# Hybrid decoder trunk on one core: down stages in whole products, the norm's end in two parts, squares on ScalarE, and the first two weight slots side by side

## The chip, the cores and the metric

The kernel runs on one core of a Trainium2 chip. The metric is device time in microseconds of one execution; the median of the runs is compared. The engines are TensorE (PE; its weight loads are listed as PEld), VectorE (DVE), ScalarE (ACT), GpSimd (POOL) and SyncE (SP), whose queue issues nearly all DMAs.

## The reference

Two layers work on x of 512 positions by 1024 features, in float32. Each layer does, in this order:

```python
x = x + 0.5 * _swiglu(_rms_norm(x, norm_ffn1[l]), ffn1_w_gate[l], ffn1_w_up[l], ffn1_w_down[l])
h = _rms_norm(x, norm_mix[l])
proj = (h @ w_in[l]).astype(jnp.float32)
# y_rwkv, y_attn, y_conv: three groups of mixers on columns of proj
mix = jnp.concatenate([y_rwkv, y_attn, y_conv], axis=-1).astype(x.dtype)
x = x + mix @ w_out[l]
x = x + 0.5 * _swiglu(_rms_norm(x, norm_ffn2[l]), ffn2_w_gate[l], ffn2_w_up[l], ffn2_w_down[l])
```

`_swiglu(x, g, u, d)` is `(silu(x @ g) * (x @ u)) @ d` with an inner width of 2816, and `_rms_norm` is `x * rsqrt(mean(x * x) + 1e-6) * gain`. The three mixers are RWKV-7 time mixing, dilated sliding-window attention and a Conformer convolution of 31 taps with a gate in front.

## The kernel before

**Layout and products.** x is kept transposed as eight tiles x[0] to x[7] of 128 features by 512 positions. A float32 product is made of three: each operand is split into a high part (hi, xh, ah) and a low remainder (lo, xl, al), and hi times xh, hi times xl and lo times xh are added up in one PSUM bank. So a column of 128 outputs over 1024 inputs takes 8 x 3 = 24 products of 128 x 128 weights with 512 positions (`mm3` in the mixer, `mms` in the FFNs). PSUM has four banks for such columns (tag "g"), two each for the tags "b" and "c".

**Weight slots.** `slot` (L107) brings one piece of weights by DMA to `raw` (3 buffers), casts it to `hi` on ScalarE (L114) and subtracts to get `lo` on VectorE (L115); hi and lo have two buffers each, so that one slot can be made ready while the products of the slot before it run.

**FFN.** `ffn` (L251) has an up stage, 22 pairs (f) of a gate and an up column, 1056 products, and a down stage, 8 output tiles of 22 x 3 = 66 products. Each pair goes through `gated` (L240): gate times R (L243, VectorE), Silu (ScalarE), up times R (L245), their product on GpSimd (L246) and the split to ah and al. `mms` (L125) takes a form for each stage from the tables UP and DOWN: "std" is the order above; "alt" has lo times xh second; "inner" and "outer" cut each product into two of 256 positions, next to each other or as two passes over the slot. In layer 0 nothing is cut. In layer 1 both down stages are: "inner" in the first FFN, "outer" in the second.

**The norm.** The factor of the norm is the same for all features of a position, so it is applied behind the product, as R. `norm_tile` (L197), called for each x tile as soon as it is final, makes xh on ScalarE (L202) and xl on VectorE (L203), squares x on GpSimd (L210; L207 for the first tile) and adds the squares up there (L211). `norm_end` (L225) then multiplies with ones on TensorE (L229), adds eps on VectorE (L215), takes the power of -0.5 on GpSimd (L216), spreads the result over the partitions by products with the identity on TensorE (L221) and copies it to R on ScalarE (L235). It is called behind the first pair of an FFN (in the very first FFN behind the third column, with the first pair held), and behind the convolution's first two columns in the mixer. That makes six ends of a norm.

**The mixer's head and end.** `columns` in `mixer` takes two convolution columns, the end of the norm, the gate (L992 to L996) and the taps (L1011, at a low priority), then the low-rank column (`finish`, L404 to L407, and `lora_in`, up to L399), then k, r and v. `first(0)` needs column k0 and the low-rank tile L (products L430 and L431). At the mixer's end, for each of the eight x tiles, nine products of the output projection are added to what is there, x is updated (L722) and `norm_tile` follows.

**Order.** A planner orders the instructions of each engine by the order of the source, by priorities and by its own estimate of when operands are ready; it can put work of a later line between. Each engine then executes its own list in order. The core starts with a DMA of the first weight slot, four x tiles, the second slot and four x tiles.

Of the kernel before, what the change touches and what calls it, by code (L numbers as in the profile page):

```python
# [41 lines left out]
NP = 3  # L42
# [41 lines left out]
class Kern:  # L84
# [39 lines left out]

    def mms(self, form, out, todo, first, last):  # L125

        mm = self.nc.tensor.matmul
        order = ((0, 2), (1, 2), (0, 3)) if form == "alt" else ((0, 2), (0, 3), (1, 2))
        n = [0]
        total = len(todo) * 3 * (1 if form in ("std", "alt") else 2)  # L130

        def one(t, w, x, s):

            mm(out[:, s], lhsT=t[w], rhs=t[x][:, s], start=first and n[0] == 0, stop=last and n[0] == total - 1, skip_group_check=True)  # L134
            n[0] += 1

        halves = (slice(0, T // 2), slice(T // 2, T))
        if form == "outer":
            for s in halves:
                for t in todo:  # L140
                    for w, x in order:
                        one(t, w, x, s)
            return
        for t in todo:
            for w, x in order:
                for s in halves if form == "inner" else (slice(0, T),):
                    one(t, w, x, s)

    def split(self, hi, lo, src):
# [33 lines left out]
    def norm_begin(self, idx):  # L183
        self.xp = self.tc.tile_pool(name=self.n("xp"), bufs=1, side="right")
        pool = self.xp.__enter__()
        xh = lambda j: pool.tile([P, T], F32R, tag=f"xh{j}", name=self.n("xh"))
        xl = lambda j: pool.tile([P, T], F32R, tag=f"xl{j}", name=self.n("xl"))
        if idx == 3:
            z = [(xh(j), xl(j)) for j in range(KT)]
            self.xh, self.xl = [a for a, b in z], [b for a, b in z]  # L190
        else:
            self.xh, self.xl = [xh(j) for j in range(KT)], [xl(j) for j in range(KT)]
        pool.tile([P, XPAD], F32, name=self.n("xpad"))
        self.nidx = idx
        self.acc = self.nrm.tile([P, T], F32, tag="acc", name=self.n("acc"))

    def norm_tile(self, j):  # L197

        nc = self.nc
        x = self.x[j]  # L200
        g = self.gains[:, self.nidx * KT + j : self.nidx * KT + j + 1]
        nc.scalar.activation(self.xh[j], x, AF.Copy, scale=g)  # L202
        nc.vector.scalar_tensor_tensor(  # L203
            self.xl[j], x, g, self.xh[j].bitcast(F32), op0=ALU.mult, op1=ALU.subtract
        )
        if j == 0:
            nc.gpsimd.tensor_tensor(self.acc, x, x, op=ALU.mult)  # L207
        else:
            sq = self.nrm.tile([P, T], F32, tag="sq", name=self.n("sq"))
            nc.gpsimd.tensor_tensor(sq, x, x, op=ALU.mult)  # L210
            nc.gpsimd.tensor_tensor(self.acc, self.acc, sq, op=ALU.add)  # L211
# [12 lines left out]

    def norm_end(self):  # L225
        nc = self.nc
        ps = self.psum("c", 2)
        for i in range(4):
            nc.tensor.matmul(ps[:, i : i + 1], lhsT=self.acc[:, i * P : (i + 1) * P], rhs=self.ones, start=True, stop=True)  # L229
# [5 lines left out]
        nc.scalar.copy(self.R, ps)  # L235
# [15 lines left out]
    def ffn(self, l, n, nxt, last=False):  # L251
        nc, I = self.nc, self.I
        with self.tc.tile_pool(name=self.n("ffn"), bufs=1) as ap, self.tc.tile_pool(name=self.n("fft"), bufs=2) as tp:
            ah, al = [], []
            held = None
            for f in range(FT):
                p = []
                for w in range(2):
                    hi, lo = self.ahead.pop(0) if self.ahead else self.slot(I["wgu"][l, n, f, w], 1024)
                    ps = self.psum()  # L260
                    cols = lambda k: slice(k * P, (k + 1) * P)
                    self.mms(UP[l, n], ps, [(hi[:, cols(k)], lo[:, cols(k)], self.xh[k], self.xl[k]) for k in range(KT)], True, True)
# [13 lines left out]
            for j in range(KT):  # L276
                ps = self.psum()
                for q in range(0, FT, 8):
                    m = min(8, FT - q)
                    hi, lo = self.slot(I["wd"][l, n, j, :, q * P : (q + m) * P], m * P)  # L280
                    cols = lambda k: slice(k * P, (k + 1) * P)
                    todo = [(hi[:, cols(k)], lo[:, cols(k)], ah[q + k], al[q + k]) for k in range(m)]
                    self.mms(DOWN[l, n], ps, todo, q == 0, q + m == FT)
                nc.vector.scalar_tensor_tensor(  # L284
# [18 lines left out]
    def mixer(self, l):  # L303
# [11 lines left out]

        der = m1.tile([P, 10 + 3 + 3 + 3 + 3 + 3 + 3], F32, name=self.n("der"))
        V.tensor_scalar(der[:, 0:10], pa("mu", 0, 10), -1.0, 1.0, op0=ALU.mult, op1=ALU.add)
# [21 lines left out]
        L = m1.tile([P, T], F32, name=self.n("L"))  # L339
        fd = m1.tile([P, NC, NP], F32, name=self.n("fd"))  # L340
        for h in range(2):
# [22 lines left out]
        def columns():  # L364

            yield from self.conv_cols(0, mt, column, zp, True)
            self.taps(0, zp, acc, mt, pa, None)
            ps = self.psum()
            yield from column(ps)
            finish(9, L, ps)  # L370
            lora_in()
            for n, q in [("k", q) for q in range(NP)] + [("r", q) for q in range(NP)] + [("v", q) for q in range(NP)]:
# [10 lines left out]
                done.add((n, q))  # L383
            yield from self.conv_cols(1, mt, column, zp, False)

# [37 lines left out]
        def first(q):  # L423
# [16 lines left out]
            for i in range(4):  # L440
                mm(ps[:, 2 * i : 2 * i + 2], lhsT=sq[:, i * P : (i + 1) * P], rhs=self.tb("hsel"), start=True, stop=True)
            sg = mt(3, [P, 2, NC, HD + 1], "sg")
            sg, cs = sg[:, 0], sg[:, 1]
# [534 lines left out]

    def conv_cols(self, u, mt, column, zp, first):
        nc = self.nc  # L980
        V, A = nc.vector, nc.scalar
        pss = [self.psum() for _ in range(2)]
        for ps in pss:
            yield from column(ps)
        if first:
            self.norm_end()
        if u == 0:
# [60 lines left out]
    def run(self):  # L1048
# [93 lines left out]
```

## Time and profile before

| | |
|---|---|
| median of 3 runs | 2122.24 us (2116.41 to 2122.78) |
| profiled execution | 2122.5 us, span 2120.7 us |
| TensorE | 2064.2 us busy, 11462 products, mean granted clock 0.985 |
| VectorE | 1164.5 us busy |
| ScalarE | 715.3 us busy |
| GpSimd | 409.3 us busy |
| DMA | 193.94 MB, mean 91 GB/s |

All rows of views come from the one profiled execution; its time stands beside its span, since a sum made from rows is a change of that execution. In the view in order of time a row has its start, its duration, engine, line, operation and tiles, and in brackets how long the engine was idle before it and what ended that. Products are pipelined, so a row's duration overlaps with the next row; the pace is read from the starts. In the view by stretches a row has the stretch, its length, then busy time and count of each engine (TensorE, weight loads, VectorE, ScalarE, GpSimd), the granted clock, the share of the DMA engines and GB/s. In the view of one line's instructions the three durations are least, median and greatest in ns. In the view of waits the three numbers are us in total, times, and the longest.

### The profile page before, as it was taken

Reading aid. Unit: us, or ns where it says so; the run is one execution under the profiler, and the core shown is the slowest. Engines: PE = TensorE matmul, PEld = TensorE weight load, DVE = VectorE, ACT = ScalarE, POOL = GpSimd, SP = SyncE. Lnnn points to the kernel's source line nnn. Section 1 sums busy time; section 2 is a strip of 40 time slices with the busy share of each in tenths; the row PEclk is TensorE's granted clock in tenths of the full one; section 3 lists DMA queues with packets and bytes.
Section 4 is the critical chain, followed back from the end, with each engine's and each line's share of the span. In section 5 each row is a group of like instructions: output and inputs, shape, how many; then the busy total and the mean of one; then the engine's idle time right before and its main releaser. Section 6 shows DMA issues by size and latency. Waiting matters only on the chain. (4 is left out here: it accounts for less than half of the span.)

```text
span 2120.7 us, 28040 instructions
## 1 busy us (share of the span) xinstructions
PE 2064.2 (97%) x11462; PEld 1714.5 (81%) x11462; DVE 1164.5 (55%) x1565; ACT 715.3 (34%) x1088; POOL 409.3 (19%) x346
## 2 busy tenths in 40 slices
PE   7999999989999999999999999999899999999999
PEld 5888888767876788888878888997688667888999
DVE  5554534698866544444445444337987764555422
ACT  3332222453355322322223232224534643323211
POOL 5111112122412311102111101222323131111000
PEclk9999999999989999999999999999999999999999
DMA  4333333212312332333323333332233132333332
GB/s 144 93 98 99 89 113 122 82 54 80 78 55 68 110 100 91 98 95 102 93 91 97 100 100 97 107 110 69 55 88 89 38 96 90 100 94 95 100 105 75
DMA packets 81873, 193.94 MB, mean 91 GB/s; under 512 B 26640, under 2 KB 32272, under 8 KB 81744
## 3 DMA queue, kind: packets, MB, share of 16 engines
q1 hardware_dynamic: 81312, 191.79, 30.0%
q8 instruction: 90, 1.47, 0.3%
q10 hardware_dynamic: 432, 0.36, 0.1%
q14 instruction: 39, 0.32, 0.0%
HBM read 183.47 MB, written 8.65 MB: 91 GB/s over the span
## 5 line engine op out<-in xcount | busy, mean ns | idle before, releaser
L114 ACT CAST hi<-raw 128x1024 fp32r<-128x1024 f32 (+3 forms) x368 | 350.7, 953 | 1042.6 <-PE psg L134 556.3
L115 DVE TENSOR_TENSOR lo<-raw,hi 128x1024 fp32r<-128x1024 f32 (+3 forms) x368 | 518.2, 1408 | 313.7 <-ACT hi L114 312.2
L134 PE MATMUL psg<-xh,hi 128*128 128x512 f32 x1408 | 549.7, 391 | 6.8 <-ACT xh L202 6.8
L134 PE MATMUL psg<-xl,hi 128*128 128x512 f32 x1408 | 550.5, 391 | 3.8 <-DVE xl L203 3.7
L134 PE MATMUL psg<-xh,lo 128*128 128x512 f32 x1408 | 549.5, 390 | 3.7 <-DVE lo L115 3.7
L134 PEld LDWEIGHTS psg<-xl,hi 128*128 128x128 f32 x1408 | 265.0, 188 | 63.2 <-DVE xl L203 8.6
L134 PEld LDWEIGHTS psg<-xh,hi 128*128 128x128 f32 x1408 | 265.1, 188 | 61.6 <-ACT xh L202 6.8
L134 PEld LDWEIGHTS psg<-xh,lo 128*128 128x128 f32 x1408 | 265.0, 188 | 59.5 <-DVE lo L115 5.0
L134 PE MATMUL psg<-al,hi 128*128 128x256 f32 (+1 forms) x1056 | 307.5, 318 | 0.0
L134 PE MATMUL psg<-ah,lo 128*128 128x256 f32 (+1 forms) x1056 | 307.5, 318 | 0.0
L134 PE MATMUL psg<-ah,hi 128*128 128x256 f32 (+1 forms) x1056 | 307.5, 318 | 0.0
L246 POOL TENSOR_TENSOR s<-s,u 128x512 f32<-128x512 f32 x88 | 114.5, 1301 | 807.5 <-ACT hi L114 449.9
L245 DVE TENSOR_TENSOR u<-psg,R 128x512 f32<-128x512 f32 x88 | 60.8, 691 | 275.4 <-PE psg L134 275.4
L134 PEld LDWEIGHTS psg<-al,hi 128*128 128x128 f32 x1056 | 188.6, 191 | 13.9
L134 PEld LDWEIGHTS psg<-ah,hi 128*128 128x128 f32 x1056 | 188.6, 191 | 13.7
L134 PEld LDWEIGHTS psg<-ah,lo 128*128 128x128 f32 x1056 | 188.6, 191 | 13.7
L243 DVE TENSOR_TENSOR g<-psg,R 128x512 f32<-128x512 f32 x88 | 60.8, 691 | 137.9 <-PE psg L134 128.1
L210 POOL TENSOR_TENSOR sq<-x 128x512 f32<-128x512 f32 x42 | 57.9, 1378 | 235.9 <-DVE x L284 232.0
L1011 DVE SCALAR_TENSOR_TENSOR cacc<-z,par,cacc 128x482 f32<-128x482 f32 (+14 forms) x120 | 96.9, 808 | 3.6 <-ACT cacc L1004 1.8
L121 PE MATMUL psg<-xh,hi 128*128 128x512 f32 x224 | 94.8, 423 | 0.0
L123 PE MATMUL psg<-xh,lo 128*128 128x512 f32 x224 | 93.8, 419 | 0.0
L122 PE MATMUL psg<-xl,hi 128*128 128x512 f32 x224 | 93.7, 419 | 0.0
(214 smaller groups left out, 2228.7 us busy)
## 6 DMA issues: line engine op xcount, KB each, us to landing
raw<-in_wgu_dram SPq DMA_DIRECT2D x176, 512.0 KB, 3.5
raw<-in_wd_dram SPq DMA_DIRECT2D x64, 512.0 KB, 3.5
raw<-in_win_dram SPq DMA_DIRECT2D x28, 512.0 KB, 3.5
raw<-in_wd_dram SPq DMA_DIRECT2D x32, 384.0 KB, 3.1
raw<-in_watt_dram SPq DMA_DIRECT2D x24, 384.0 KB, 3.1
raw<-in_wout_dram SPq DMA_DIRECT2D x28, 192.0 KB, 2.4
xs<-x SPq DMA_DIRECT2D x16, 256.0 KB, 2.0
x<-xs SPq DMA_DIRECT2D x16, 256.0 KB, 3.0
```

The source lines that it names most:

```text
L114: nc.scalar.copy(hi[:, :cols], raw[:, :cols])
L115: nc.vector.tensor_tensor(lo[:, :cols], raw[:, :cols], hi[:, :cols].bitcast(F32), op=ALU.subtract)
L121: mm(out, lhsT=whi, rhs=xhi, start=first, stop=False)
L122: mm(out, lhsT=whi, rhs=xlo, start=False, stop=False)
L123: mm(out, lhsT=wlo, rhs=xhi, start=False, stop=last)
L134: mm(out[:, s], lhsT=t[w], rhs=t[x][:, s], start=first and n[0] == 0, stop=last and n[0] == total - 1, skip_group_check=True)
L210: nc.gpsimd.tensor_tensor(sq, x, x, op=ALU.mult)
L243: nc.vector.tensor_tensor(t[0], p[0], self.R, op=ALU.mult)
L245: nc.vector.tensor_tensor(t[1], p[1], self.R, op=ALU.mult)
L246: nc.gpsimd.tensor_tensor(t[2], t[2], t[1], op=ALU.mult)
L1011: nc.vector.scalar_tensor_tensor(a[:, d:], z[:, 0 : T - d], pa("dww", u * CW + j), a[:, d:], op0=ALU.mult, op1=ALU.add)
```

## The change

- The forms are gone. Every FFN column uses `mm3` with whole products of 512 positions in the order hi xh, hi xl, lo xh.
- `norm_end` becomes `norm_sum` (up to the power) and `norm_spread` (spread and R). In every FFN the sum follows the first pair and the spread follows the next column, 24 products later; the first pair is held and goes through `gated` together with the second. In the mixer the sum follows the two convolution columns, then the low-rank column is computed, then come the spread, the gate, the finish of the low-rank column and the taps.
- `norm_tile` squares on ScalarE; GpSimd only adds.
- At the start the order of DMAs is slot, x[0], slot, x[1] to x[7], and the first pair's two columns are computed together: six products for each x tile.
- Some tiles are padded (`der`, `fd`, `sg`), the reserved scratch area at the start of SBUF has 2048 bytes for each partition instead of the default, and the xh and xl tiles of one norm (index 3) are allocated in the same order as the others. These move addresses of tiles.

```diff
-UP = {(0, 0): "std", (0, 1): "alt", (1, 0): "std", (1, 1): "std"}
-DOWN = {(0, 0): "std", (0, 1): "alt", (1, 0): "inner", (1, 1): "outer"}
+SCRATCH = 2048
...
         if j == 0:
-            nc.gpsimd.tensor_tensor(self.acc, x, x, op=ALU.mult)
+            nc.scalar.activation(self.acc, x, AF.Square)
         else:
             sq = self.nrm.tile([P, T], F32, tag="sq", name=self.n("sq"))
-            nc.gpsimd.tensor_tensor(sq, x, x, op=ALU.mult)
+            nc.scalar.activation(sq, x, AF.Square)
             nc.gpsimd.tensor_tensor(self.acc, self.acc, sq, op=ALU.add)
...
-    def norm_end(self):
+    def norm_sum(self):
         nc = self.nc
         ps = self.psum("c", 2)
         for i in range(4):
             nc.tensor.matmul(ps[:, i : i + 1], lhsT=self.acc[:, i * P : (i + 1) * P], rhs=self.ones, start=True, stop=True)
         self.rn = self.rnt
         self.rsqrt(self.rn, ps[:, 0:4], EPS)
+
+    def norm_spread(self):
+        nc = self.nc
         ps = self.psum("c", 2)
         self.spread(ps, self.rn)
...
+                if f == 0 and l == 0 and n == 0:
+
+                    both = [self.ahead.pop(0) for w in range(2)]
+                    p = [self.psum() for w in range(2)]
+                    for k in range(KT):
+                        for (hi, lo), ps in zip(both, p):
+                            s = slice(k * P, (k + 1) * P)
+                            self.mm3(ps, hi[:, s], lo[:, s], self.xh[k], self.xl[k], k == 0, k == KT - 1)
+                    self.norm_sum()
+                    held = p
+                    continue
                 for w in range(2):
                     hi, lo = self.ahead.pop(0) if self.ahead else self.slot(I["wgu"][l, n, f, w], 1024)
                     ps = self.psum()
...
-                    if (f, w) == ((1, 0) if l == 0 and n == 0 else (0, 1)):
-                        self.norm_end()
-                if f == 0 and l == 0 and n == 0:
+                    if (f, w) == (0, 1):
+                        self.norm_sum()
+                    elif (f, w) == (1, 0):
+                        self.norm_spread()
+                if f == 0:
                     held = p
                     continue
...
-            yield from self.conv_cols(0, mt, column, zp, True)
-            self.taps(0, zp, acc, mt, pa, None)
+            pss = [self.psum() for _ in range(2)]
+            for ps in pss:
+                yield from column(ps)
+            self.norm_sum()
             ps = self.psum()
             yield from column(ps)
+            self.norm_spread()
+            self.conv_gate(0, mt, pss, zp)
             finish(9, L, ps)
+            self.taps(0, zp, acc, mt, pa, None)
             lora_in()
...
-            if j in (0, 4):
-                self.ahead.append(self.slot(I["wgu"][0, 0, 0, j // 4], 1024))
+            if j in (0, 1):
+                self.ahead.append(self.slot(I["wgu"][0, 0, 0, j], 1024))
```

More of the change, by code (lines that the diff above doesn't have):

```diff
@@ L123, in mm3 @@
         mm(out, lhsT=wlo, rhs=xhi, start=False, stop=last)
[L125 to L147, printed above, removed]
     def split(self, hi, lo, src):
@@ L187, in norm_begin @@
         xl = lambda j: pool.tile([P, T], F32R, tag=f"xl{j}", name=self.n("xl"))
[L188 to L192, printed above, removed]
+        self.xh, self.xl = [xh(j) for j in range(KT)], [xl(j) for j in range(KT)]
         pool.tile([P, XPAD], F32, name=self.n("xpad"))
@@ L260, in ffn @@
                     ps = self.psum()
-                    cols = lambda k: slice(k * P, (k + 1) * P)
-                    self.mms(UP[l, n], ps, [(hi[:, cols(k)], lo[:, cols(k)], self.xh[k], self.xl[k]) for k in range(KT)], True, True)
+                    for k in range(KT):
+                        s = slice(k * P, (k + 1) * P)
+                        self.mm3(ps, hi[:, s], lo[:, s], self.xh[k], self.xl[k], k == 0, k == KT - 1)
                     p.append(ps)
-                    if (f, w) == ((1, 0) if l == 0 and n == 0 else (0, 1)):
-                        self.norm_end()
-                if f == 0 and l == 0 and n == 0:
+                    if (f, w) == (0, 1):
[3 more added lines that the diff above has]
+                if f == 0:
                     held = p
@@ L280, in ffn @@
                     hi, lo = self.slot(I["wd"][l, n, j, :, q * P : (q + m) * P], m * P)
-                    cols = lambda k: slice(k * P, (k + 1) * P)
-                    todo = [(hi[:, cols(k)], lo[:, cols(k)], ah[q + k], al[q + k]) for k in range(m)]
-                    self.mms(DOWN[l, n], ps, todo, q == 0, q + m == FT)
+                    for k in range(m):
+                        s = slice(k * P, (k + 1) * P)
+                        self.mm3(ps, hi[:, s], lo[:, s], ah[q + k], al[q + k], q + k == 0, q + k == FT - 1)
                 nc.vector.scalar_tensor_tensor(
@@ L314, in mixer @@
         mt = lambda j, sh, nm, dt=F32: mx.tile(sh, dt, tag=f"m{j}", name=self.n(nm))
-        der = m1.tile([P, 10 + 3 + 3 + 3 + 3 + 3 + 3], F32, name=self.n("der"))
+        der = m1.tile([P, 64], F32, name=self.n("der"))
         V.tensor_scalar(der[:, 0:10], pa("mu", 0, 10), -1.0, 1.0, op0=ALU.mult, op1=ALU.add)
@@ L339, in mixer @@
         L = m1.tile([P, T], F32, name=self.n("L"))
-        fd = m1.tile([P, NC, NP], F32, name=self.n("fd"))
+        fd = m1.tile([P, 64], F32, name=self.n("fd"))[:, 0 : NC * NP].rearrange("p (c q) -> p c q", q=NP)
         for h in range(2):
@@ L383, in columns @@
                 done.add((n, q))
-            yield from self.conv_cols(1, mt, column, zp, False)
+            pss = [self.psum() for _ in range(2)]
+            for ps in pss:
+                yield from column(ps)
+            self.conv_gate(1, mt, pss, zp)
         def step(n):
@@ L441, in first @@
                 mm(ps[:, 2 * i : 2 * i + 2], lhsT=sq[:, i * P : (i + 1) * P], rhs=self.tb("hsel"), start=True, stop=True)
-            sg = mt(3, [P, 2, NC, HD + 1], "sg")
+            sg = mt(3, [P, 17 * HD], "sg")[:, 0 : 2 * NC * (HD + 1)].rearrange("p (x c t) -> p x c t", x=2, c=NC)
             sg, cs = sg[:, 0], sg[:, 1]
@@ L977, in att_core, with conv_gate @@
                 yield 1
-    def conv_cols(self, u, mt, column, zp, first):
+    def conv_gate(self, u, mt, pss, zp):
         nc = self.nc
         V, A = nc.vector, nc.scalar
[L982 to L986, printed above, removed]
         if u == 0:
@@ L1130 @@
     A = arrays({k: np.asarray(v) for k, v in inputs.items()})
-    nc = _bacc.Bacc("TRN2", target_bir_lowering=False, num_devices=1)
+    nc = _bacc.Bacc("TRN2", target_bir_lowering=False, num_devices=1, dynamic_dma_scratch_size=SCRATCH)
     feed, I = {}, {}
```

## The prediction

> **What bounds the kernel now.** I read the page first, for the engine that has no room left.
>
> ```profile
> span 2120.7 us, 28040 instructions
> ...
> PE 2064.2 (97%) x11462; PEld 1714.5 (81%) x11462; DVE 1164.5 (55%) x1565; ACT 715.3 (34%) x1088; POOL 409.3 (19%) x346
> ...
> PEclk9999999999989999999999999999999999999999
> ```
>
> TensorE is busy for 97% of the span, the next engine for 55%. So time can be had in two ways only: make TensorE's own work shorter, or take away the 56 us in which it stands and the few slices in which its clock is down. Second, the chain of waits in order of time. Its last stretch is the whole second FFN of layer 1, and the only thing in it that isn't a product is one end of the norm:
>
> ```profile
> 1759.12 1.95 POOL rnt L216
> ...
> 1762.27 354.78 PE psg L134 x2062
> ```
>
> **Uncut down stages.** The busy time by stretches has one row for each down stage. The first row is the first down stage of layer 0, uncut; the others are layer 1's two, the stages that the diff changes.
>
> ```profile
> 260.30:380.00 119.70, 119.70 (x529) 99.10 (x528) 51.33 (x40) 28.56 (x33) 21.49 (x14) 1.00 0.36 111
> 1305.00:1431.80 126.80, 126.80 (x1054) 126.62 (x1054) 45.96 (x44) 28.70 (x34) 24.95 (x19) 1.00 0.35 108
> 1990.16:2117.05 126.89, 126.87 (x1057) 126.66 (x1055) 33.29 (x32) 23.00 (x24) 1.29 (x1) 1.00 0.30 91
> ```
>
> All three compute 8 x 22 x 3 = 528 products of 512 columns, at clock 1.00, with TensorE never idle. Uncut they start 119.70/528 = 0.2267 us apart; cut there are 1056 of 256 columns, 0.1202 apart. A cut product pays its fixed share twice: 2 x 0.1202 - 0.2267 = 0.0137 us, times 528 is 7.2 us. Both stages take the uncut form, so **-7.1 - 7.2 = -14.3 us**. Weights stay ahead: the uncut stage asks for them only 6% faster, and the first row shows that it never waited for them. This is the surest term; bounds 13.5 to 14.5.
>
> The Trainium skill (TensorE: Matmul & The Clock Gate, section "Wait — 56ns, not 53.3ns?") puts the fixed cost of a warm product at about 2.5 ns. An estimate by that page is 2 x 528 x 0.0025 = 2.6 us for both stages in place of 14.3. The rows have 13.7 ns for it, so the measurement decides.
>
> **The norm's end in two parts.** At each of the six ends of the norm the products of ones with the sum of squares (L229), the power on GpSimd (L216) and the spread (L221) wait for one another in a row, with two products between in TensorE's queue. The first of the six:
>
> ```profile
> 31.91 0.95 PE L229 MATMUL psc<-ones,acc 128*128 128x1 f32 x8
> 32.71 0.49 PE L134 MATMUL psg<-xh,hi 128*128 128x512 f32 x1
> ...
> 35.13 1.16 PE L221 MATMUL psc<-tab,rnt 128*128 128x128 f32 x8 [1.69 <-POOL rnt L216]
> 36.04 0.67 PE L134 MATMUL psg<-xh,lo 128*128 128x512 f32 x1
> 36.51 0.63 PE L134 MATMUL psg<-xh,hi 128*128 128x512 f32 x1
> 36.93 0.63 PE L134 MATMUL psg<-xl,hi 128*128 128x512 f32 x1
> ```
>
> The sum takes 0.80 us of TensorE, the spread 0.91; both stay. What goes is the standstill of 1.69 us between them, and what follows it: products now start 0.43 us apart, not 0.227, because the clock fell. The waits of all six, and the three stretches of 8.1 us in which the clock fell, are:
>
> ```profile
> PE psc L221 <- POOL rnt L216: 9.2, 6, 1.7
> ```
>
> ```profile
> 31.91:40.01 8.10, 6.41 (x30) 0.79 0.26 77
> 391.09:399.22 8.13, 6.43 (x29) 0.79 0.22 66
> ...
> 1441.82:1449.92 8.10, 6.41 (x29) 0.79 0.21 65
> ```
>
> Idle 9.2 us in all; clock (1 - 0.79) x 8.1 = 1.7 us in each of three, 5.1 us. In the changed kernel a whole slot of products, 24 x 0.2267 = 5.44 us, lies between sum and spread. The chain that it must cover is L229's end to the spread: 35.13 - 32.71 = 2.4 us. If the DVE's small addition stands behind a conversion of a weight slot (1.23 us, below) it is 3.7 us, still under 5.44. So I take all of it: **-14.3 us**. Bounds: -9.2 (the clock falls for another reason) to -16 (the records of the products' ends hide about 0.2 us of each standstill).
>
> The Trainium skill (same page, section "What's actually happening") says that the clock falls after an idle window of about 3.4 us. By that rule pauses of 1.7 us would cost no clock and this term would be 9.2 us. The rows show three of six pauses with the clock at 0.79 over 8.1 us, so I keep 14.3.
>
> **First two slots side by side.** The start, from the view in order of time:
>
> ```profile
> 5.76 1.23 DVE L115 TENSOR_TENSOR lo<-raw,hi 128x1024 fp32r<-128x1024 f32 x1 [4.89 <-ACT hi L114]
> ...
> 6.83 0.79 PE L134 MATMUL psg<-xh,hi 128*128 128x512 f32 x1 [6.83 <-ACT xh L202]
> ...
> 10.47 1.04 ACT L114 CAST hi<-raw 128x1024 fp32r<-128x1024 f32 x1 [1.48 <-DMA raw<-in_wgu_dram]
> ...
> 12.93 2.31 DVE L115 TENSOR_TENSOR lo<-raw,hi 128x1024 fp32r<-128x1024 f32 x1
> ...
> 15.16 6.35 DVE L203 SCALAR_TENSOR_TENSOR xl<-x,gains,xh 128x512 fp32r<-128x512 f32 x4
> ...
> 26.46 0.39 PE L134 MATMUL psg<-xh,hi 128*128 128x512 f32 x1
> ```
>
> Now the first slot's 24 products crawl behind DVE, which makes one xl in 1.59 us (6.35/4) and is done at 21.5; the second slot's 24 then run at full pace, and the third slot starts at 26.46. In the changed kernel each arriving x tile feeds six products (1.36 us), so both slots end about six products after the last xl. The second slot's DMA is queued before x1 rather than before x4. Its cast then comes around 8 to 9 us (an estimate: by now three x tiles and this slot, 1.25 MB, land between 6.0 and 10.47, so 256 KB each 0.9 us), and TensorE stands at the fourth product until then, and at the sixth until DVE has lo, near 10.5. Then 42 products remain: 9.5 us, about 2 more for a clock still low: 22. If DVE stays at 1.59 us a tile it ends near 22.5 and TensorE near 23.5. One new wait: both pairs of hi and lo buffers are in use until the end, so the third slot's cast (1.04) and lo (1.23) can't run ahead; the sum (0.80) and two products cover all but 0.5 us. I take 22.5: **-4 us**; bounds -1.4 (every xl at 1.77 us, the slowest below) and -6.3 (products alone: 6.83 + 10.9 + 2).
>
> **Squares on ScalarE.** GpSimd loses one of its two operations for each of 48 tiles, ScalarE gains one. It costs:
>
> ```profile
> L1027 ACT ACTIVATE z<-cacc x4: 630/631/631, 603.8 to 1652.6; 128x512 f32<-128x512 f32 x4
> ```
>
> ```profile
> 411.16 0.71 ACT L438 ACTIVATE tmp<-k,par 128x512 f32<-128x512 f32 x1
> ...
> 413.91 1.28 ACT L455 ACT_TABLE_LOAD   x1
> ```
>
> 0.63 us each, 48 x 0.63 = 30 us on an engine that is busy for 34%. It needs no new table: L438 is a square and ran before the reload at 413.91. In the down stages this changes nothing for TensorE (28.6 of 119.7 us busy). Where it counts is the mixer's end, with nine products for each x tile:
>
> ```profile
> 685.69:700.30 14.61, 11.34 (x44) 7.43 (x43) 14.61 (x15) 6.11 (x10) 13.89 (x10) 1.00 0.50 150
> 1733.38:1752.20 18.82, 15.49 (x60) 10.53 (x59) 18.43 (x17) 7.07 (x11) 17.88 (x13) 1.00 0.50 147
> ```
>
> ```profile
> 1739.65 1.24 POOL L210 TENSOR_TENSOR sq<-x 128x512 f32<-128x512 f32 x1
> 1739.91 1.52 DVE L203 SCALAR_TENSOR_TENSOR xl<-x,gains,xh 128x512 fp32r<-128x512 f32 x1
> 1740.96 1.62 POOL L211 TENSOR_TENSOR acc<-acc,sq 128x512 f32<-128x512 f32 x1
> 1741.36 0.68 DVE L722 TENSOR_TENSOR x<-psg,x 128x512 f32<-128x512 f32 x1
> 1741.96 1.04 DVE L115 TENSOR_TENSOR lo<-raw,hi 128x384 fp32r<-128x384 f32 x1
> 1742.07 0.72 ACT L202 ACTIVATE xh<-x,gains 128x512 fp32r<-128x512 f32 x1 [1.89 <-DVE x L722]
> ```
>
> DVE is full and needs 3.0 us a tile, TensorE nine products, 2.1 us. DVE is slow because GpSimd works beside it: over the run its xl takes
>
> ```profile
> L203 DVE SCALAR_TENSOR_TENSOR xl<-x,gains,xh x48: 737/1528/1778, 6.9 to 1750.3; 128x512 fp32r<-128x512 f32 x48
> ```
>
> 0.74 us at best. TensorE's idle time here is 14.61 - 11.34 = 3.3 us and 18.82 - 15.49 = 3.3 us; by starts (59 steps of 0.2333 are 13.8 of 18.8) it is 5. GpSimd keeps its addition, so DVE gets to about 2.5 us a tile, halfway between 3.0 and the 1.9 of undisturbed operations. ScalarE's load is 0.49 + 0.72 + 0.63 = 1.84, just under TensorE's 2.1. I take 2.5 us for each layer, **-5 us**; bounds 0 and -10.
>
> **The mixer's head.** The first R now comes after a third column, and the convolution's gate and the low-rank column both follow it.
>
> ```profile
> 396.24 0.59 ACT L235 COPY R<-psc 128x512 f32<-128x512 f32 x1 [4.13 <-PE psc L221]
> ...
> 406.38 0.42 DVE L399 TENSOR_SCALAR L<-L 64x512 f32<-64x512 f32 x1
> ...
> 408.18 0.69 PE L431 MATMUL psb<-L,lora 32*128 32x512 f32 x1
> ```
>
> The sum would start at 391.09 as now; plus 0.8, a column of 5.44, the spread 0.9 and R 0.59 makes R ready at 398.8, 2 us later than now, while TensorE itself is 4 us earlier. Gate (2.2 us) and finish put L near 405.6; TensorE could want it at 403.7. The column after it has 24 products to put in between, and three stand there already, so most is covered: **+1 us** for two layers. If that cover is gone: 1.9 us idle and 1.7 of clock in each, 7.2. Bounds 0 and +7.2.
>
> The larger pads and the smaller scratch area move addresses and issue no instruction: 0, with the case under the rivals as its bound.
>
> **The sum.** 14.3 + 14.3 + 4 + 5 - 1 = 36.6. The profiled execution took 2122.5 us, 1.8 beside its span, and the median of the runs shown is 2122.24, the same within 0.02%. So **2086 us**, 1.7% faster.
>
> **Rivals.** (a) *The wait goes to the four product banks.* In three FFNs the first pair is now held as in the first, so four tiles are held when the fifth is due. If the pair's DVE operations are queued behind the second pair's, TensorE stands for one of them (0.7) and pays 1.7 of clock, 2.4 us three times: 2093. For: it is a real dependence. Against: R is there 1.5 us into a slot of 5.44, and the first FFN held a pair already without such a wait. (b) *The mixer's head isn't covered*: +6 more, 2092. (c) *The planner pulls the spread forward* to where it stands now, so that the split does nothing: 2100. Against: it put two products between the parts that the source writes as one, so it fills and does not hurry. (d) *Slower: the new addresses.* In the output projection, products of the same size start further apart:
>
> ```profile
> 1725.68:1733.38 7.70, 7.70 (x34) 6.19 (x33) 5.82 (x9) 3.34 (x6) 4.02 (x3) 1.00 0.39 101
> ```
>
> 7.70/33 = 0.2333, with TensorE never idle. If the shift brought the 6336 FFN products to that pace they would cost 6336 x 0.0066 = 42 us: 2128. It decides from about 87% of them on. Against: both up and down stages run at 0.2267 with operands in some hundred tiles.
>
> **How the numbers follow.** Forecast 0.77, with its own range 2076 to 2096; (a) 0.09, (b) 0.06, (c) 0.04, (d) 0.02; 0.02 for a gain that vanishes in a way I don't see. The bounds of all terms together reach from 2075 to 2105; I give 2074 to 2103. About 0.3% (6.4 us) is what a measurement of this kernel can tell from no change. Only (d) and the last case are not beyond it: faster 0.96, same 0.02, slower 0.02.
>
> **What would show it.** Right: layer 1's down stages at 119.7 us with 528 products; no wait of L221 for L216 and a clock of 1.00 behind each norm; the third slot's first product near 22.5 us; DVE with idle time at the mixer's end. Wrong: a wait of products for L243, of L431 for L399, a start later than 25 us, or a pace of 0.233 in the FFNs. Over 2103 would mean that a wait has taken the place of the norm's.

## The result and the profile after

The changed kernel takes 2083.94 us (median, 2081.86 to 2084.98) where the kernel before, run beside it, takes 2120.78: ratio 0.983, interval 0.981 to 0.985. 2086 was forecast, with 2074 to 2103. The total is right, but terms of the sum were off in both directions and their errors cancel; most of what follows is about those.

The page of the changed kernel, the lines that answer to those of before:

```profile
span 2080.1 us, 25896 instructions
...
PE 2031.8 (98%) x10406; PEld 1653.1 (79%) x10406; DVE 1121.5 (54%) x1565; ACT 740.0 (36%) x1136; POOL 330.4 (16%) x298
```

TensorE has 1056 products fewer (two down stages uncut), GpSimd is 79 us less busy, ScalarE 25 us more. The lead of the changed kernel, read at the starts of the same work in both profiles:

| place | before, us | after, us | lead | gained since the row above |
|---|---|---|---|---|
| first x update of layer 0's first down stage | 275.5 | 275.0 | 0.5 | 0.5 |
| sum of the norm in layer 0's mixer | 391.1 | 390.4 | 0.7 | 0.2 |
| first low-rank product of `first(0)` (mixer's head) | 408.2 | 403.9 | 4.3 | 3.6 |
| convolution's mean (mixer's middle) | 599.6 | 596.2 | 3.4 | -0.9 |
| first x update of the output projection | 624.0 | 617.0 | 7.0 | 3.6 |
| sum of the next norm | 709.7 | 698.4 | 11.3 | 4.3 |
| first x update of layer 0's second down stage | 956.2 | 943.9 | 12.3 | 1.0 |
| the same, layer 1's first down stage | 1320.0 | 1304.8 | 15.2 | 2.9 |
| its last x update | 1430.9 | 1409.5 | 21.4 | 6.2 |
| mixer of layer 1: sum | 1441.8 | 1420.2 | 21.6 | 0.2 |
| first low-rank product | 1458.9 | 1433.8 | 25.1 | 3.5 |
| convolution's mean | 1648.9 | 1623.6 | 25.3 | 0.2 |
| first x update of the output projection | 1671.9 | 1644.4 | 27.5 | 2.2 |
| sum of the next norm | 1757.9 | 1725.8 | 32.1 | 4.6 |
| first x update of the last down stage | 2006.2 | 1971.3 | 34.9 | 2.8 |
| last x update | 2117.1 | 2076.1 | 41.0 | 6.1 |

The two rows on each of layer 1's down stages hold its first output tile (0.9) and the rest (6.1 or 6.2). The profiled execution of before was 1.7 us above its median and that of after 2.1 below, hence 41.0 here against 36.8 between the medians. The rows between the first low-rank product and the first x update of the output projection, the body of a mixer (-0.9 + 3.6 and 0.2 + 2.2), belong to these two executions rather than to the change, as the experiment on uncut stages alone and the last section show.

The down stages of layer 1, busy time by stretches, changed kernel:

```profile
1289.70:1409.40 119.70, 119.70 (x530) 99.17 (x529) 39.15 (x40) 32.26 (x40) 12.35 (x7) 1.00 0.36 110
1956.20:2075.90 119.70, 119.70 (x529) 98.96 (x527) 33.29 (x32) 23.10 (x24) 1.29 (x1) 1.00 0.32 96
```

119.7 us each, as forecast to the tenth. The end of the norm in layer 0's mixer, in order of time (start, duration):

```profile
390.37 0.94 PE L199 MATMUL psc<-ones,acc 128*128 128x1 f32 x8
391.17 0.49 PE L119 MATMUL psg<-xh,hi 128*128 128x512 f32 x1
...
396.76 1.05 PE L191 MATMUL psc<-tab,rnt 128*128 128x128 f32 x8
...
398.11 0.39 PE L121 MATMUL psg<-xh,lo 128*128 128x512 f32 x1
398.34 0.40 PE L119 MATMUL psg<-xh,hi 128*128 128x512 f32 x1
```

The spread (L191, L221 before) has no idle time in front of it, and behind it products start 0.23 us apart. The first FFN is another matter. Its start in order of time, TensorE:

```profile
21.09 0.39 PE L121 MATMUL psg<-xh,lo 128*128 128x512 f32 x1
25.23 1.05 PE L199 MATMUL psc<-ones,acc 128*128 128x1 f32 x8 [3.75 <-POOL acc L181]
26.15 0.54 PE L119 MATMUL psg<-xh,hi 128*128 128x512 f32 x1
26.48 0.63 PE L120 MATMUL psg<-xl,hi 128*128 128x512 f32 x1
28.56 2.08 PE L191 MATMUL psc<-tab,rnt 128*128 128x128 f32 x8 [1.45 <-POOL rnt L186]
30.29 0.78 PE L121 MATMUL psg<-xh,lo 128*128 128x512 f32 x1
```

and on ScalarE and GpSimd, two of the squares and additions behind it:

```profile
14.46 0.64 ACT L180 ACTIVATE sq<-x 128x512 f32<-128x512 f32 x1 [0.50 <-POOL acc L181]
```

```profile
15.17 1.62 POOL L181 TENSOR_TENSOR acc<-acc,sq 128x512 f32<-128x512 f32 x1 [0.74 <-ACT sq L180]
17.53 1.62 POOL L181 TENSOR_TENSOR acc<-acc,sq 128x512 f32<-128x512 f32 x1 [0.74 <-ACT sq L180]
```

Both columns end at 21.3, earlier than the 22 of the forecast. But then TensorE waits 3.75 us for the sum of squares, 1.45 us for the power two products later, and goes on at half pace (products 0.43 us apart behind the spread). Squares and additions take turns, since there is one buffer for a square.

The mixers' ends (before: 14.61 us with TensorE busy for 11.34, 18.82 with 15.49) and xl's times over the run:

```profile
674.00:688.60 14.60, 14.04 (x60) 10.85 (x59) 14.25 (x19) 11.53 (x20) 8.20 (x6) 1.00 0.62 183
1701.40:1720.20 18.80, 18.25 (x79) 14.28 (x79) 17.55 (x22) 12.80 (x22) 9.86 (x7) 1.00 0.57 179
```

```profile
L173 DVE SCALAR_TENSOR_TENSOR xl<-x,gains,xh x48: 739/746/1787, 7.1 to 1718.5; 128x512 fp32r<-128x512 f32 x48
```

TensorE is busy for 14.04 of 14.60 us, and xl's median is 0.75 us, down from 1.53. VectorE is still nearly full (14.25 us): in the last tiles of the first layer the x updates start 2.23 us apart, where the prediction took 2.5 and nine products take 2.1, so VectorE and TensorE are now close to even there.

### The profile page after: what moved, and what is told of

The parts are those of the page before. It is cut to its first block, busy times and chain, and to the rows that moved or that the text cites. A ratio compares the mean times of both kernels' runs of the same rounds, so it can differ in the third digit from the quotient of the medians.

```text
span 2080.1 us, 25896 instructions
## 1 busy us (share of the span) xinstructions
PE 2031.8 (98%) x10406; PEld 1653.1 (79%) x10406; DVE 1121.5 (54%) x1565; ACT 740.0 (36%) x1136; POOL 330.4 (16%) x298
## 4 chain that ended last, share of the span: by engine, by line
PE 86%; DVE 8%; POOL 2%; issue 2%; ACT 2%; DMA 0%; SPq 0%; POOLq 0%; ACTq 0%; DVEq 0%
PE psg L119 25%; PE psg L121 25%; PE psg L120 25%; DVE lo L113 2%; DVE cacc L1001 1%; PE psg L915 1%; DVE Ei L584 1%; PE psb L485 1%; DVE tm L578 1%; PE psc L950 1%; PE psg L867 1%; POOL ast L895 1%; PE psg L941 1%; POOL acc L181 1%; PE psg L869 1%
## 5 line engine op out<-in xcount | busy, mean ns | idle before, releaser
L120 PE MATMUL psg<-al,hi 128*128 128x512 f32 x704 | 274.2, 389 | 0.0
L119 PE MATMUL psg<-ah,hi 128*128 128x512 f32 x704 | 274.2, 389 | 0.0
L121 PE MATMUL psg<-ah,lo 128*128 128x512 f32 x704 | 274.2, 389 | 0.0
L121 PEld LDWEIGHTS psg<-ah,lo 128*128 128x128 f32 x704 | 132.2, 188 | 27.6
L119 PEld LDWEIGHTS psg<-ah,hi 128*128 128x128 f32 x704 | 132.2, 188 | 27.4
L120 PEld LDWEIGHTS psg<-al,hi 128*128 128x128 f32 x704 | 132.2, 188 | 27.1
L181 POOL TENSOR_TENSOR acc<-acc,sq 128x512 f32<-128x512 f32 x42 | 68.4, 1628 | 379.8 <-ACT sq L180 379.8
L124 ACT CAST ah<-s 128x512 fp32r<-128x512 f32 x88 | 54.9, 624 | 113.1 <-POOL s L219 113.1
L867 PE MATMUL psg<-hi,xh 128*128 128x384 f32 x192 | 68.7, 358 | 2.5 <-ACT nat L892 2.5
L868 PE MATMUL psg<-lo,xh 128*128 128x384 f32 x192 | 65.1, 339 | 0.0
```

Of the source, the lines that this page charges most:

```text
L119: mm(out, lhsT=whi, rhs=xhi, start=first, stop=False)
L120: mm(out, lhsT=whi, rhs=xlo, start=False, stop=False)
L121: mm(out, lhsT=wlo, rhs=xhi, start=False, stop=last)
L867: mm(o, lhsT=self.xh[kk][:, t], rhs=hi[:, s], start=kk == 0, stop=False)
L868: mm(o, lhsT=self.xh[kk][:, t], rhs=lo[:, s], start=False, stop=False)
```

## The experiments

Medians in us. The kernel before was run beside each group: 2120.65 for the first four, 2119.64 for the next four, 2118.29 for the last three.

| kernel | median | ratio to before | interval |
|---|---|---|---|
| changed kernel | 2083.94 | 0.983 | 0.981 to 0.985 |
| changed, squares on GpSimd | 2100.12 | 0.991 | 0.990 to 0.993 |
| changed, old start | 2080.27 | 0.982 | 0.980 to 0.984 |
| changed, two buffers for squares in the first norm | 2079.26 | 0.981 | 0.980 to 0.983 |
| changed, old addresses | 2084.47 | 0.984 | 0.982 to 0.985 |
| changed, norm's end joined | 2097.51 | 0.990 | 0.988 to 0.991 |
| two buffers, and the first norm's end held in place | 2075.89 | 0.979 | 0.978 to 0.981 |
| old start and two buffers | 2080.34 | 0.981 | 0.980 to 0.983 |
| before, uncut alone | 2105.93 | 0.993 | 0.991 to 0.994 |
| before, split alone | 2112.39 | 0.996 | 0.995 to 0.998 |
| before, squares alone | 2106.83 | 0.995 | 0.993 to 0.997 |
| before, start alone | 2123.68 | 1.002 | 1.001 to 1.003 |

### Squares back on GpSimd

```diff
-            nc.scalar.activation(sq, x, AF.Square)
+            nc.gpsimd.tensor_tensor(sq, x, x, op=ALU.mult)
```

(The first tile likewise.)

> The changed kernel with the squares back on GpSimd, all else as changed. Theory: at the two mixers' ends GpSimd's square beside DVE is what made DVE the bound, and moving it gave 4.3 and 4.6 us there (the lead over the kernel before grows by that much between the first x update of the output projection and the sum of the next norm); in the first FFN the sum of squares would be ready near 27 us instead of 25.2, 2 us more. So 2083.9 + 8.9 + 2 = 2095 us, with DVE full again at both mixers' ends. Rival: the mixers gained from new addresses or another order of the planner, and the squares do nothing: 2084 to 2086 us.

Measured: 2100.12, 16 more than the changed kernel, 5 more than the theory said. The mixer's end, busy time by stretches, and xl:

```profile
684.00:699.00 15.00, 11.76 (x46) 7.80 (x46) 15.00 (x15) 6.49 (x10) 14.21 (x11) 1.00 0.48 150
```

```profile
L173 DVE SCALAR_TENSOR_TENSOR xl<-x,gains,xh x48: 737/1759/1777, 6.9 to 1738.3; 128x512 fp32r<-128x512 f32 x48
```

VectorE is full again and TensorE stands for 3.2 us of 15. From the first x update of the output projection to the next sum it takes 85.8 us in both layers, as before (85.8 and 86.0), against 81.4 in the changed kernel: 4.4 us a layer, 8.8 in all where the theory had 8.9. The first FFN is 5.0 us later, not 2, since the sum now waits 5.7 us for the squares. The mixers' middles made up most of the rest of its profile (22.6 and 24.1 us instead of 20.8); that belongs to the execution and not to the edit, as the last section shows.

### The old start

```diff
-            if j in (0, 1):
-                self.ahead.append(self.slot(I["wgu"][0, 0, 0, j], 1024))
+            if j in (0, 4):
+                self.ahead.append(self.slot(I["wgu"][0, 0, 0, j // 4], 1024))
```

The branch of `ffn` that computes the first two columns together is left out.

> The changed kernel with the start of the kernel before: second weight slot behind four x tiles, first two columns one after the other, the sum behind the second column and the spread behind the third as in the other FFNs. Theory: side by side the 48 products end at 21.3 us instead of 26.5, but the sum of squares is not ready until 25.2 and the spread then stands close behind it, so that the first FFN as a whole gained 0.5 us; with the old start the sum finds its squares ready and the spread is covered, which gives the 3.7 us of the first norm: 2083.9 - 3 = 2081 us. Rival: the side by side start is worth the 4 us that were forecast: 2088 us.

Measured: 2080.27, 3.7 us better than the changed kernel in the median; the ranges overlap, since one of its four runs took 2085.90. The gain is plain in the profile, where the first x update of the down stage comes at 271.5 us instead of 275.0. TensorE, in order of time:

```profile
21.15 0.39 PE L121 MATMUL psg<-xh,lo 128*128 128x512 f32 x1
24.31 1.05 PE L199 MATMUL psc<-ones,acc 128*128 128x1 f32 x8 [2.77 <-POOL acc L181]
...
32.40 1.05 PE L191 MATMUL psc<-tab,rnt 128*128 128x128 f32 x8
```

The 48 products end at 21.4, with the columns one after the other. What made them earlier than before (26.5) is VectorE's faster xl, and not their order. The sum still waits for its squares, against the theory, since the columns got that much faster; the spread is covered. So side by side costs about 3.5 us in the first FFN. The reading that fits both traces is that both pairs of hi and lo buffers stay in use until its end and the planner fills the gap before the third column's lo with the spread; why the planner placed it there was not tested apart.

### Two buffers for the squares of the first norm

```diff
-            sq = self.nrm.tile([P, T], F32, tag="sq", name=self.n("sq"))
+            sq = self.nrm.tile([P, T], F32, tag=("sq", "R")[j % 2 if self.nidx == 0 else 0], name=self.n("sq"))
```

> The changed kernel with two buffers for the squares in the first norm (the tile of R, which is free there, takes every other one). Theory: ScalarE's squares and GpSimd's additions alternate because there is one buffer (0.74 us of GpSimd idle before each addition); with two the additions run back to back, 10.2 + 7 x 1.6 = 21.5 us, and TensorE's wait for the sum falls from 3.8 us to under 1: about 2081 us. The wait of the spread (1.45 us) and the slow clock behind it stay. Rival: GpSimd's additions get slower as they crowd DVE's work, or the third slot's cast sets the pace: 2083.5 to 2084.5 us.

Measured: 2079.26, 4.7 us better. GpSimd, then TensorE, in order of time:

```profile
10.40 12.03 POOL L181 TENSOR_TENSOR acc<-acc,sq 128x512 f32<-128x512 f32 x7 [8.72 <-ACT sq L180]
```

```profile
22.88 0.94 PE L199 MATMUL psc<-ones,acc 128*128 128x1 f32 x8
...
26.10 2.08 PE L191 MATMUL psc<-tab,rnt 128*128 128x128 f32 x8 [1.70 <-POOL rnt L186]
27.83 0.77 PE L121 MATMUL psg<-xh,lo 128*128 128x512 f32 x1
28.41 0.63 PE L119 MATMUL psg<-xh,hi 128*128 128x512 f32 x1
```

Seven additions in a row, no wait of the sum; the spread's wait and the half pace behind it stay, as the theory had it. A part of the rival shows as well: beside additions back to back seven xl take 10.93 us on VectorE instead of 7.83, and the two columns end at 22.9 us instead of 21.3. The first x update comes at 271.9 us, 3.1 earlier than in the changed kernel.

### The old addresses

`der`, `fd`, `sg`, the scratch area and the order of allocation as in the kernel before; the instructions are the same.

> The changed kernel with the paddings, the scratch area and the allocation order of the kernel before: same instructions, other addresses. Theory: addresses cost nothing, 2084 +- 2 us, and the FFN products start 0.2267 us apart. Rival: the 2.2 to 3.6 us that each mixer gained in its middle (beyond the norm at its head and the end of the output projection) come from the addresses: 2083.9 + 5.8 = 2090 us.

Measured: 2084.47, within the changed kernel's range, and the eight x updates of each down stage start 14.96 us apart as there (66 products at 0.2267). Addresses cost nothing that can be measured, and rival (d) of the prediction falls with them. Every engine has the same list of instructions as in the changed kernel, in the same order, and yet the mixers' middles take 21.5 and 21.4 us in this profile where they took 20.8 in the other.

### The norm's end joined

```diff
-                    if (f, w) == (0, 1):
+                    if (f, w) == ((1, 0) if l == 0 and n == 0 else (0, 1)):
                         self.norm_sum()
-                    elif (f, w) == (1, 0):
                         self.norm_spread()
```

In the mixer the spread, the gate and the taps go back in front of the low-rank column, and only the first FFN holds a pair.

> The changed kernel with the two parts of the norm's end joined again at their old places (in the first FFN behind the third column). Theory: each of the later five ends loses what it lost in the kernel before, 3.7 + 1.1 + 2.0 + 3.7 + 2.0 = 12.5 us, of which 5.0 is clock, and the first FFN gains back about 3 us, because its sum comes a column later and finds its squares: 2083.9 + 12.5 - 3 = 2093 us. Rival (the clock does not hang on these pauses): idle time alone, 1.7 + 0.8 + 3 x 1.7 = 7.6 us, less 3: 2088.5 us.

Measured: 2097.51, 13.6 more than the changed kernel. The first FFN gained nothing back: the planner put the sum in front of the third column all the same, with 3.6 us of wait. The later five ends cost 12.7 in the profile. Stretches of 8.1 us from the sum on, TensorE only:

```profile
390.60:398.70 8.10, 6.40 (x36) 1.00 0.23 65
700.20:708.30 8.10, 6.41 (x37) 1.00 0.19 67
1063.00:1071.10 8.10, 6.41 (x36) 1.00 0.20 65
1425.90:1434.00 8.10, 6.41 (x30) 0.79 0.18 65
1737.30:1745.40 8.10, 6.41 (x30) 0.79 0.21 67
```

All five have the same pause of 1.7 us. The clock falls behind two of them; in the kernel before it fell behind the first, second and fifth of six, so at the head of layer 0's mixer there and not here, and in the last FFN here and not there. The last section shows what decides it.

### Two buffers, and the first norm's end held in place

Beside the two buffers, in the first FFN only:

```diff
+                        if (l, n, f, w, k) == (0, 0, 1, 0, 2):
+                            with self.tc.issue_after(self.pm.ins):
+                                self.norm_sum()
...
                     elif (f, w) == (1, 0):
-                        self.norm_spread()
+                        with self.tc.issue_after(self.pm.ins):
+                            self.norm_spread()
```

`self.pm` is the last product of `mm3`; the call of the sum behind the first pair goes.

> The changed kernel with two buffers for the squares of the first norm, and in the first FFN alone the sum tied behind the ninth product of the third column and the spread behind its last, so that the planner can't pull them forward. Theory: with two buffers alone the spread still stands two products behind the sum and waits 1.7 us, and the clock falls behind it; with 15 products (3.4 us) between them both go: 3 us below the version with two buffers alone, 2079.3 - 3 = 2076 us. Rival: the third column's weights, which can't be made ready earlier, set the pace there, and the planner was right: 2079 to 2080 us.

Measured: 2075.89, as the theory said, 8 us below the changed kernel and the fastest of all (ratio to before 0.979, interval 0.978 to 0.981). TensorE, in order of time:

```profile
25.71 0.39 PE L121 MATMUL psg<-xh,lo 128*128 128x512 f32 x1
25.94 0.95 PE L199 MATMUL psc<-ones,acc 128*128 128x1 f32 x8
...
30.07 0.39 PE L121 MATMUL psg<-xh,lo 128*128 128x512 f32 x1
30.29 1.05 PE L191 MATMUL psc<-tab,rnt 128*128 128x128 f32 x8
```

No wait at either part, and full pace behind both: the clock stays at 1.00 from 23 us to 430 us. The first x update comes at 269.0 us, 2.9 earlier than with two buffers alone.

### The old start and two buffers

The edits of the two experiments, together.

> The changed kernel with the old start (one column after the other) and two buffers for the squares of the first norm. Theory: the old start's 48 products end at 21.15 us, no later than side by side, since DVE is no longer slowed by squares on GpSimd; only the sum's wait of 2.8 us is left, and the two buffers take it and the slow clock behind it: 2080.3 - 3.5 = 2077 us. Rival: the additions on GpSimd slow DVE again when they run back to back, and the first columns end later: 2080 us.

Measured: 2080.34, the same as with the old start alone, and the number of the rival. At the start the rival is what happened: beside additions back to back VectorE's last four xl take 6.86 us instead of 4.79, and the 48 products end at 23.6 us instead of 21.4. But the sum then finds its squares and the clock doesn't fall, so that over the first FFN the theory holds in its size: the first x update of the down stage comes at 269.1 us, as early as in the fastest kernel (269.0), against 271.5 with the old start alone. In these two profiles the 2.4 us are lost again in the middles of the mixers, from the convolution's mean to the first x update of the output projection. TensorE there, first with the old start and two buffers:

```profile
590.60:613.30 22.70, 22.29 (x227) 0.85 0.09 25
1619.90:1641.50 21.60, 21.14 (x227) 0.92 0.08 25
```

and with the old start alone:

```profile
592.70:613.50 20.80, 19.65 (x226) 1.00 0.08 27
1620.20:1641.00 20.80, 19.64 (x227) 1.00 0.09 26
```

The two kernels have the same list of instructions on every engine, in the same order, but for the first FFN. So the same products take 20.8 us at clock 1.00 or up to 22.7 us at 0.85. The edit didn't do that, as the next experiment shows: such differences come from one execution to the next.

### Uncut alone

```diff
-DOWN = {(0, 0): "std", (0, 1): "alt", (1, 0): "inner", (1, 1): "outer"}
+DOWN = {(0, 0): "std", (0, 1): "alt", (1, 0): "std", (1, 1): "std"}
```

> The kernel before with nothing but whole products in its two cut down stages. Theory: each stage falls from 126.9 to 119.7 us and nothing else moves: 2120.7 - 14.2 = 2106.5 us. Rival: the stage before or after takes some back, or the clock in the mixer's middle falls elsewhere: up to 4 us either way, 2102 to 2111 us, with the down stages at 119.7 all the same.

Measured: 2105.93, 13.7 less than before, and the two stages at 119.7 us:

```profile
1300.50:1420.20 119.70, 119.70 (x529) 99.12 (x529) 51.33 (x40) 28.55 (x32) 21.48 (x14) 1.00 0.36 110
1982.80:2102.50 119.70, 119.70 (x529) 98.97 (x528) 33.29 (x32) 23.12 (x24) 1.29 (x1) 1.00 0.32 96
```

This kernel's two mixers have the same instructions in the same order as those of the kernel before, and the down stage of layer 1's first FFN is the first thing that differs. Yet from the first low-rank product to the first x update of the output projection layer 0's mixer is 3.0 us shorter here and layer 1's 3.1 us longer, with clocks that fell at other places. A difference of 3 us in the body of a mixer is therefore no sign that an edit did something.

### Split alone, squares alone, start alone

Each is the kernel before with one part of the change: the norm's end in two parts; the squares on ScalarE; the DMA order and the branch for the first two columns.

> The kernel before with nothing but the norm's end in two parts (sum behind the first pair in all FFNs, spread a column later; in the mixer a column between). Theory: the later five ends save 12.5 us as the joined version showed (12.8 in its profile), the first one up to 3.7, less a short wait for squares that are ready near 27 us: 2120 - 15.5 = 2104.5 us. Rival: in the mixers' heads and the FFNs the held pair costs something that the other parts hide: 2108 to 2110 us.

> The kernel before with nothing but the squares on ScalarE. Theory: 4.4 us at each mixer's end, and in the first FFN xl takes 0.75 us instead of 1.55, so that its first two columns end near 21.2 us instead of 26.5, while the sum, a column later, finds its squares: 2120 - 8.8 - 5.2 = 2106 us. Rival: ScalarE's 30 us more make the weight slots late, or the start isn't bound by VectorE: 2111 us (the mixers' ends alone).

> The kernel before with nothing but the first two weight slots side by side (DMA order and products); the norm's end still written behind the third column. Theory: the planner pulls the end of the norm in front of the third column, the squares on GpSimd aren't ready until about 29 us, and what the columns gain is lost in that wait: 2120 + 4 = 2124 us. Rival: the forecast of the document, 4 us gained: 2116 us.

Measured: 2112.39 (5.9 less than before), 2106.83 (11.5 less) and 2123.68 (5.4 more, interval 1.001 to 1.003). Their sums of the norm, first FFN, in order of time, split alone and then start alone:

```profile
29.34 1.05 PE L229 MATMUL psc<-ones,acc 128*128 128x1 f32 x8 [3.00 <-POOL acc L211]
```

```profile
22.74 0.39 PE L123 MATMUL psg<-xh,lo 128*128 128x512 f32 x1
28.86 1.87 PE L229 MATMUL psc<-ones,acc 128*128 128x1 f32 x8 [5.74 <-POOL acc L211]
```

Split alone, the sum comes a column earlier than before and waits 3.0 us for squares that GpSimd has not made; the first x update comes 1.1 us later than before instead of up to 3.7 earlier, while the later five ends gain 11.9 us in its profile. Together that is 10.8 us, and its last x update is 10.6 us earlier than before. The medians show less, 5.9 (interval 5 to 11): the profiled execution of the kernel before, at 2122.5 us, was 4.2 slower than the median of the 25 runs beside this group. Squares alone took the 2106 us of the theory, but the kernel before ran at 2118.29 beside it and not at the 2120 that the theory starts from, so the gain is 11.5 and not 14. Start alone ends its columns near 23 us, about 3.5 earlier than before, and loses it and more by waiting 5.7 us for the squares: the only part that made the kernel slower.

## Why the prediction was right, and where it was wrong

The forecast was 2086, and 2083.94 was measured. By its steps:

- **Uncut down stages, -14.3: right.** 119.7 us for each, 13.7 us less when done alone. The page of the Trainium skill (TensorE: Matmul & The Clock Gate, section "Wait — 56ns, not 53.3ns?") would have made it 2.6, an estimate; the rows had the price in this kernel.
- **The norm's end, -14.3: right for five of six.** The later five gained 12.0 us in the profile (3.6, 1.0, 2.0, 3.5, 1.9) where their share of the term was 10.9, and joining them cost 12.7. The sixth, in the first FFN, gained nothing: "I take all of it" missed that the planner could move the spread there, which is rival (c), priced for all ends at 0.04 and met at one. That side by side keeps both weight buffers busy, which would explain it, stands in the same prediction under another heading. The 5.1 us of clock in the term were those of one execution: the clock fell behind three of its six pauses, and behind others in other profiles.
- **First two slots, -4: wrong, they cost 3.7 in the medians and 3.5 in the rows of the first FFN.** The step that failed is "both slots end about six products after the last xl", read as a gain: they did end at 21.3, but the sum that follows wants the sum of squares, and that was at 25.2. The step priced ScalarE's and VectorE's work at the start and left out the chain from square to addition with one buffer. And the earlier end was not its own: with the columns one after the other it is 21.4, because xl is faster. The gain belonged to the next term.
- **Squares on ScalarE, -5: right in its mechanism, too small.** The mixers' ends gained 8.9 us (4.3 and 4.6) of the 10 that were to be had. VectorE's tile was put at 2.5 us, halfway; it came to 2.23, close to TensorE's 2.1. The sign that was named, VectorE with idle time at the mixer's end, hardly shows: it is busy for 14.25 of 14.60 us. With the start counted in, the squares were worth 16 us in the changed kernel and 11.5 alone.
- **The mixer's head, +1: it cost nothing.** From the sum to the first low-rank product it takes 13.5 us, 3.6 less than before, the whole of the pause and the clock.
- **Not in the sum, and rightly so:** the mixers' middles, 3.6 and 2.2 us in the two profiles, where the same products ran at clock 0.80 and 0.85 before:

```profile
599.60:624.00 24.40, 23.98 (x226) 0.80 0.08 23
1648.90:1671.90 23.00, 22.30 (x227) 0.85 0.08 25
```

and at 1.00 in the changed kernel:

```profile
596.20:617.00 20.80, 19.65 (x227) 1.00 0.09 27
1623.60:1644.40 20.80, 19.65 (x225) 1.00 0.07 26
```

It looks like a gain of the change and is a difference between two executions: split alone has a middle of 20.8 us too, in its first mixer, and the changed kernel's own list of instructions, at the old addresses, took 21.5 and 21.4.

So the start and the first norm gave 0.5 us instead of 7.4 (4 for the start and 1.7 + 1.7 for the first norm's pause and clock). Against these 6.9 us stand 3.9 more at the mixers' ends (8.9 - 5), 1.1 more at the later ends of the norm and 1 at the mixers' heads, 6.0 together. Without the mixers' bodies, 5.1 us, the rows add up to about 36 us, near the 36.6 of the sum and the 36.8 of the medians. The total was right by luck as much as by its steps. Rivals (a) and (b) did not show: there is no wait of products for the gate of the held pair, nor of the low-rank product for L.

## What to carry to other kernels

When a stage is freed, ask what its next step waits for: the earlier end of the first columns was worth nothing until the sum of squares came earlier as well, and one more buffer did that. A part that only fills a gap (the side by side start) can cost the cover that another part needs; price such edits together, and undo each in the finished kernel, since alone and in place, by the medians, they were worth 5.9 and 13.6 us (split), 11.5 and 16.2 (squares), -5.4 and -3.7 (start). Where a planner orders the work, a split in the source may not hold unless its order is tied down: with two buffers, holding the first norm's end in place was worth 3.4 us, and both together 8. And before a few us between two profiles are put down to an edit, look at where the clock fell in each: in the mixers here that alone moved 3 us either way.

## What the runs showed of the hardware

A pause of 1.7 us of TensorE lowered the clock in some places and not in others, with the same busy time of 6.4 in 8.1 us around it: behind three of six ends in the kernel before, two of five in the joined version, and at different ends of the norm. What decides it can be read from the traces, which keep the moments at which the granted clock falls and comes back. In each of the 13 profiles all of these moments lie on one grid of steps of 3.413 us: in the kernel before the clock falls at 36.15, 394.55 and 1445.86 us, 105 and 413 steps behind the first, and it stays at 0.5 for one step or for a few. The grid goes on through the whole execution, whatever the kernel does, and lies elsewhere against the start in each profile. The pauses of 1.7 us against this grid:

| kernel | pause begins, us | behind the last step of the grid, us | clock |
|---|---|---|---|
| before | 33.43 | 0.69 | falls |
| before | 392.62 | 1.48 | falls |
| before | 1073.23 | 2.84 | stays |
| before | 1443.34 | 0.90 | falls |
| before | 1759.42 | 2.95 | stays |
| joined | 392.14 | 0.05 | stays |
| joined | 701.72 | 2.43 | stays |
| joined | 1064.55 | 0.03 | stays |
| joined | 1427.38 | 1.05 | falls |
| joined | 1738.82 | 1.87 | falls |

Two of the joined version's ends, step by step (TensorE only):

```profile
392.09:395.50 3.41, 1.71 (x12) 1.00 0.46 121
395.50:398.91 3.41, 3.41 (x16) 1.00 0.08 32
1426.33:1429.74 3.41, 1.72 (x13) 1.00 0.09 20
1429.74:1433.15 3.41, 3.41 (x12) 0.50 0.34 133
```

With the three other kernels whose ends of the norm are joined (uncut alone, squares alone, start alone) there are 24 such pauses that begin at full clock. The clock fell behind all 11 that began 0.69 to 2.15 us into a step and behind none of the 13 that began before 0.53 or after 2.41. So the place of a pause on the grid decides. That is a window of fixed length that runs on by itself, as the Trainium skill has it (TensorE: Matmul & The Clock Gate, section "What's actually happening"), and the traces agree with its length of about 3.4 us. They differ from it in what makes the clock fall, since the page of the Trainium skill asks for an idle window of that length and half of one was enough here; the measurement decides. Why a pause that begins at once in a step is harmless, and why the clock fell in the mixers behind steps in which TensorE was busy throughout (from 592.53 us in the kernel before), stays open.

The mixers' bodies follow from this. Their middles took 20.8 us in every profile in which the clock stayed at 1.00 there, and 21.4 to 24.7 in the others. No kernel was profiled twice, so that the grid lies elsewhere in each execution of one kernel is read from the times: 25 runs of the kernel before took 2113.6 us at a mean granted clock of 0.989 to 2125.3 at 0.983, the longer the lower the clock.

VectorE's xl took 0.74 us when no work of GpSimd on 128x512 was under way at its start, and longer when one was, a square or an addition alike: 45 of 48 took 1.12 to 1.78 us in the kernel before. In the changed kernel only 7 did (1.60 to 1.79 us, each with an addition under way); the other 41 took at most 0.75, though an addition began during 35 of them. Without the squares GpSimd is seldom at work when an xl starts, and that is where VectorE's time came from.
